# A hybrid decoder layer on one core: the second head of a recurrent chain in its own PSUM bank, three attention steps later, and the receptance-key product at the start of a stage

## The chip, the cores and the metric

The kernel runs on one core of a Trainium2 chip. The metric is the device time of one execution in microseconds (us). TensorE (PE) multiplies matrices from SBUF into PSUM, which has eight banks of 512 fp32 values for each of 128 rows; VectorE (DVE) and ScalarE (ACT) empty PSUM; GpSimd (POOL) does small element-wise work; SyncE (SP) issues most transfers.

## The reference

A decoder layer over 512 tokens and 16 meta tokens, width 1024, in fp32. The parts that matter here are the RWKV-7 time mixing and the windowed attention, which are merged by gates:

```python
proj = h @ w_in[l]
q, k, v, zr, gate_att, gate_rwkv = jnp.split(proj, [...], axis=-1)
att = lax.map(lambda qkv: swa_one(..., sinks_l), (q, k, v))       # scores + bias, softmax with a sink, times v
rw = rwkv7_time_mix(zr, ...)
merged = jax.nn.sigmoid(gate_att) * att + jax.nn.sigmoid(gate_rwkv) * rw
...
# inside rwkv7_time_mix, 16 heads of 64, for each token:
S = S * w_t + (S @ -kk_t) (kk_t * a_t)^T + v_t k_t^T ;  y_t = S @ r_t
bonus = jnp.sum(rh * kh * r_k, -1, keepdims=True) * vh            # receptance times keys
y = (groupnorm(y) * lnx_g + lnx_b + bonus) * g
```

After the merge come `w_out`, a normalization, a squared-ReLU MLP of width 4096 and a last normalization.

## The kernel before

Every fp32 matrix is split into a rounded part and a remainder, so a product is three matmuls (`three`, lines 340 to 342). The input projection is cut into *units* of 128 columns (keys, receptances, values, query, two gates of one pair of heads); a unit is a generator that issues matmuls into one of two banks `dps` and hands each finished bank to an `evict` function.

The 16 heads are worked on as 8 pairs, one pair per *stage*, the first head of a pair in rows 0 to 63 and the second in rows 64 to 127. The recurrence is cut into 8 chunks of 64 tokens. A stage s carries, interleaved with the units of the pairs ahead:

- the *solve* of pair s-1: filling up the inverses (`rwkv_blocks`, bank tag `Y`), the meta tokens' state (`rwkv_start`, bank tag `ch`), folding (`rwkv_fold`), then the *chain*, seven steps that carry the state from chunk to chunk (`rwkv_chain`), the outputs (`rwkv_outputs`, bank tag `Y`) and the norm;
- the *scan* of pair s: scores of keys and receptances (`rwkv_scores`), the inverse of 16x16 blocks on VectorE (`rwkv_inverse`, tiles `ftmp` and `Xf`), the bonus (`rwkv_bonus`, matmuls `bp`, lines 608 and 609), turns of scores, keys and values;
- the projections of pair s+1 (`rwkv_begin`, `rwkv_lora`, tiles `tw` and `ta`), the attention scores of pair s-1 (`attention_scores`, matmuls `sp`), the gate product (`gate_out`, matmuls `gp`) and, in stages 1 and 5, the turned attention values of a new group (`turn_heads`, matmuls `vp`).

A step of the chain multiplies two matrices, one per head (line 948), and `follow` scales the results into the next state Z: the first head on VectorE (line 906), the second on ScalarE (line 908). Both halves are in one bank, `ch`.

`weave` sets the order of TensorE's work: each item has a due time in microseconds of dense matmuls since the stage began, and units are stepped until that time is reached. TensorE's order is as written (`manual_schedule`). The order on the other engines is made when the program is built, by priority among what is ready; `ahead(n)` raises the priority. The order within an engine is then fixed, and each engine works in order.

The banks: two `dn` (units), two `pg` (tag `g`), one `ch`, one `Y`, two `pat` (tag `a`). Tag `a` serves `rwkv_lora`, `turn_heads`, the attention scores and the gate product in turn. In SBUF, `at` holds tiles for the attention: the split query `qhi` and `qlo` have the tags `sph` and `spl`, with one buffer each, and `sph` also holds the split keys and the values `va` of the attention early on. `evict` of `aside_query` writes qhi on ScalarE (line 1071) and qlo on VectorE (line 1072); four transfers take them to `qs`.

At the end of the receptance unit `rwkv_reads` makes the product rk (line 594, VectorE), its rounded part rkh (line 599, ScalarE) and the remainder rkl (line 600, VectorE); `rwkv_bonus` reads them in the next stage.

Of the kernel before, what the change touches and what calls it, by code (L numbers as in the profile page):

```python
# [11 lines left out]
F32 = mybir.dt.float32  # L12
F32R = mybir.dt.float32r
I32 = mybir.dt.int32
AF = mybir.ActivationFunctionType
ALU = mybir.AluOpType
# [4 lines left out]
P = 128  # L21
D = 1024
KT = D // P
SEQ = 512
NMETA = 16
T = SEQ + NMETA
# [3 lines left out]
C = 64  # L30
NCH = SEQ // C
# [50 lines left out]
PS = (2, 2, 1, 1, 2)  # L82
# [48 lines left out]
def hybrid_layer_kernel(ctx: ExitStack, tc: tile.TileContext, I: dict, out: bass.AP):  # L131
    nc = tc.nc
    dve, act, pool, pe = nc.vector, nc.scalar, nc.gpsimd, nc.tensor
# [6 lines left out]
    pch = ppr.enter_context(tc.tile_pool(name="pch", bufs=1, space=PSUM, side="right"))  # L140
# [3 lines left out]
    @contextmanager  # L144
    def ahead(n):

        now = tc.cur_priority
        tc.cur_priority = now - n
        yield
        tc.cur_priority += n  # L150
# [48 lines left out]
    def vcol(name, j):  # L199
        return vc[:, ROW0[name] + j : ROW0[name] + j + 1]  # L200
# [203 lines left out]
    at = p2.enter_context(tc.tile_pool(name="at", bufs=1))  # L404
    pew = ctx.enter_context(ExitStack())
    ew = pew.enter_context(tc.tile_pool(name="ew", bufs=1))
# [58 lines left out]
    ER = [slice(0, 64), slice(64, 128)]  # L465
# [120 lines left out]
    def rwkv_reads(j, r):  # L586
        S = SS[j]
        AXg = S["AX"].rearrange("p c k e t -> p e c k t")
        rx = c64(r)
        for e in range(2):  # L590
            R = slice(e * HD, (e + 1) * HD)
            dve.tensor_tensor(AXg[R, e, :, 1, :], rx[R], S["Px"][R, :, 1:], op=ALU.mult)
        rk = ew.tile([P, SEQ], F32, name="rk", tag="rk")
        dve.scalar_tensor_tensor(
            rk, r[:, NMETA:], vcol("r_k", j), S["kp"][:, NMETA:], op0=ALU.mult, op1=ALU.mult
        )
        rkh = ew.tile([P, SEQ], F32R, name="rkh", tag="rkh")
        rkl = ew.tile([P, SEQ], F32R, name="rkl", tag="u")
        act.copy(rkh, rk)
        dve.tensor_tensor(rkl, rk, rkh.bitcast(F32), op=ALU.subtract)  # L600
        S["rk"] = rkh, rkl
# [298 lines left out]
    def follow(S, c, src, last):  # L900

        Z, PC = S["Z"], S["PC"]
        for e in range(2):
            dst, scale = Z[c][ER[e], e, :], PC[ER[e], last : last + 1]
            if e == 0:
                dve.tensor_scalar(dst, src[ER[e]], scale, None, op0=ALU.mult)  # L906
            else:
                act.activation(dst, src[ER[e]], AF.Copy, scale=scale)  # L908

    def rwkv_start(j, n):  # L910

        S = SS[j]
        if n == 0:
            S["meta"] = pch.tile([P, 512], F32, name="meta", tag="ch", bufs=PS[2])
            S["RHm"] = rw.tile([NMETA, 2, HD], F32, name="RHm", tag="RHm", bufs=2)
        ps, RHm = S["meta"], S["RHm"]
        p6 = [ps[:, q * C : (q + 1) * C] for q in range(6)]
        m = slice(0, NMETA)
        with ahead(PRI["start"]):
            if n == 0:  # L920
                for e in range(2):
                    pe.matmul(
                        p6[e][m], S["AKm"][:, e, :], S["SVm"][:, e, :], start=True, stop=True
                    )
                act.copy(RHm.rearrange("p e i -> p (e i)"), ps[m, 0 : 2 * C])
            if n == 1:
                for e in range(2):
                    pe.matmul(p6[2 + e][m], S["XTm"][:, e, :], RHm[:, e, :], start=True, stop=True)
                for e in range(2):
                    act.copy(S["SVm"][32 * e : 32 * e + NMETA, e, :], p6[2 + e][m])  # L930
            if n == 2:
                for e in range(2):
                    pe.matmul(
                        p6[4][ER[e]], S["BTm"][:, e, :], S["SVm"][:, e, :], start=True, stop=True
                    )
                follow(S, 0, p6[4], NCH)

    def rwkv_chain(j, c):

        S = SS[j]  # L940
        Z, GQ = S["Z"], S["AX"]
        if c == 0:
            ch = pch.tile([P, 512], F32, name="ch", tag="ch", bufs=PS[2])
            S["st"] = [ch[:, d * C : (d + 1) * C] for d in range(NCH)]
        st = S["st"]
        with ahead(PRI["chain"]):
            for e in range(2):
                pe.matmul(st[c][ER[e]], GQ[:, c, 0, e, :], Z[c][:, e, :], start=True, stop=True)  # L948
            follow(S, c + 1, st[c], c)

    def rwkv_outputs(j):
# [319 lines left out]
    for n, pools in enumerate((((dn, "dn"), (pat, "a")), ((pg, "g"), (pch, None)))):  # L1271
        for b in range(4):
            pool_, tag = pools[b // 2]
# [44 lines left out]
    SS = [{} for j in range(PAIRS)]  # L1318
# [8 lines left out]
    def reads(j):  # L1327
        unit(f"r{j}", COL_R + j * P, shifted(COL_R + j * P, j, "r", partial(rwkv_reads, j), RSP))
# [35 lines left out]
    j = PAIRS - 1  # L1364
# [18 lines left out]
    F = partial  # L1383

    def scan(j):

        need = (f"k{j}", f"r{j}", f"v{j}")
        return [
            (0.0, need, F(rwkv_scores, j, 0)),
            (3.2, (), F(rwkv_meta, j)),  # L1390
            (3.2, (), F(rwkv_scores, j, 1)),
            (3.2, (), F(rwkv_inverse, j)),
            (5.6, (), F(rwkv_bonus, j)),
            (12.4, (), F(rwkv_turn_scores, j)),
            (18.6, (), F(rwkv_turn_keys, j)),
            (16.0, (), F(rwkv_inverse_place, j)),
            (23.2, (), F(rwkv_turn_values, j)),
        ]
# [19 lines left out]
    def project_in(j):  # L1418
        return [
            (0.0, (), F(rwkv_begin, j)),  # L1420
            (7.4, (), F(rwkv_lora, j, 0)),
            (8.6, (), F(rwkv_lora, j, 1)),
            (25.5 if j == 1 else 18.6, (f"k{j}",), F(rwkv_sums, j)),
        ]

    def attend(j, t0):
        return [(t0, (f"q{j}",), F(attention_scores, j, 0))] + [
            (t0 + t, (), F(attention_scores, j, 1 + i)) for i, t in enumerate((0.0, 2.8, 4.4))
        ]

    def attend_out(j, t0, t1, t2):
        return [
            (t0, (), F(attention_turn, j, 0)),
            (t1, (), F(attention_out, j, 0)),
            (t1, (), F(attention_turn, j, 1)),
            (t2, (f"ga{j}",), F(attention_out, j, 1)),
        ]

    def join(j, t0, t1, t2):
        return [  # L1440
            (t0, (f"gr{j}",), F(gate_out, j)), (t1, (), F(merge_rwkv, j)), (t2, (), F(merge, j)),
        ]

    with tc.manual_schedule(engines={mybir.EngineType.PE}):
        for s in range(-1, PAIRS + 1):
            if s <= PAIRS:
                units[:] = [u for u in all_units[: marks[s + 1]] if u[0] not in finished]
            items = []
            if s > 0:
                items += solve(s - 1)  # L1450
            if 0 <= s < PAIRS:
                items += scan(s)
            if s == -1:
                items += [
                    (0.0, (), F(rwkv_begin, 0)),
                    (9.0, ("wa",), F(rwkv_lora, 0, 0)),
                    (10.4, (), F(rwkv_lora, 0, 1)),
                    (20.0, ("k0",), F(rwkv_sums, 0)),
                ]
            if 0 <= s < PAIRS - 1:  # L1460
                items += project_in(s + 1)
            if s == 0:
                items += [(18.0, ("av",), F(aside_heads, 0))]
            if s == 4:
                items += [(26.0, (), F(aside_heads, 1))]
            if s in (1, 5):
                items += [(8.6, (), turn_heads)]
            if 0 < s < PAIRS - 1:
                items += attend(s - 1, 9.2) + join(s - 1, 11.6, 25.4, 0)[:2]
            if 1 < s < PAIRS:  # L1470

                items += attend_out(s - 2, 0.0, 4.6, 6.4) + join(s - 2, 0, 0, 7.0)[2:]
            if s == PAIRS - 1:
                items += [(10.0, (), merged_before)]
                items += attend(s - 1, 10.0) + attend_out(s - 1, 20.5, 22.9, 25.3)
                items += join(s - 1, 11.6, 26.5, 26.5)
                items += attend(s, 16.5)
                items += [(27.2, (), F(load_out, q, 0)) for q in range(3)]
            if s == PAIRS:
                items += attend_out(s - 1, 3.0, 5.4, 7.8) + join(s - 1, 0.0, 24.5, 25.5)  # L1480
                items += [(2.0, (), F(merged, s - 2)), (25.6, (), F(merged, s - 1))]
                items += [(3.0, (), residual_gain), (17.0, (), first_up)]
                items += [(3.0 + 3 * b, (), F(residual_rows, b)) for b in range(4)]
            weave(items, True)
# [182 lines left out]
    for half in range(2):  # L1667
# [14 lines left out]
        for n in range(2):  # L1682
            ns = slice(n * 512, (n + 1) * 512)
            acc = project(half * NF, NF, fhi, flo, n, HOLD if half and n else 2, ffp)
            for b in range(4):
                dve.scalar_tensor_tensor(
                    res[b][:, ns], res[b][:, ns], 1.0 if half else ALPHA, acc[b],
                    op0=ALU.mult, op1=ALU.add,
# [58 lines left out]
```

## Time and profile before

| | |
|---|---|
| median of 3 runs | 985.71 us (983.71 to 985.78) |
| profiled execution | 984.06 us, span 982.3 us |
| TensorE busy | 940.8 us, 96% |
| VectorE busy | 655.2 us, 67% |
| ScalarE busy | 455.7 us, 46% |
| GpSimd busy | 47.8 us, 5% |
| chain that ended last | PE 72%, DVE 17%, ACT 4%, DMA 2% |

How to read the views: a timeline row has the start, the duration, the engine, the line and operation, what is written from what, and in brackets the idle time of the engine before it with the instruction that ended it. A row of the waits has the total, the number of times and the longest. Matmul durations are modelled and overlap; two matmuls follow one another at the distance of their starts.

### The profile page before, as it was taken

The page shows a single profiled execution, that of the slowest core. Times are in us where ns is not written, and L with a number is a line of the kernel's source. Part 1 is how long each engine was busy: PE and PEld are TensorE (multiplying, and loading weights), DVE is VectorE, ACT ScalarE, POOL GpSimd, SP SyncE. Part 2 cuts the span into 40 slices and gives each one's busy share as a digit, 9 for nine tenths or more (in the row PEclk, how much of TensorE's full clock was granted, in tenths as well). Part 3 has the DMA queues.
Part 4 walks back from the last instruction along what each step waited for, and adds up shares of the span by engine and source line. Part 5 has one row for each costly group of instructions (what it writes and reads, how often), then busy time and mean ns, then how long its engine had stood idle before and what let it go on. Part 6 is the DMA issues. An engine that isn't in the chain of part 4 may idle for free.

```text
span 982.3 us, 19147 instructions
## 1 busy us (share of the span) xinstructions
PE 940.8 (96%) x7557; PEld 787.7 (80%) x7557; DVE 655.2 (67%) x1505; ACT 455.7 (46%) x1130; POOL 47.8 (5%) x108
## 2 busy tenths in 40 slices
PE   4989999999999999999998999999999999999996
PEld 3889878788887887887876778988888888888885
DVE  8677888877977788778876957566423244452427
ACT  6636457465474654745736724644321133432220
POOL 2001000010000100100001001000000000000001
PEclk9999999999999999999999999999999999999998
DMA  7546323223333332242434635133322323222222
GB/s 273 95 130 166 86 75 103 79 71 109 87 91 100 104 98 79 65 111 78 144 108 105 206 119 214 44 129 107 104 89 91 103 87 107 86 95 98 79 94 85
DMA packets 82674, 105.47 MB, mean 107 GB/s; under 512 B 47766, under 2 KB 54664, under 8 KB 82584
## 3 DMA queue, kind: packets, MB, share of 16 engines
q1 hardware_dynamic: 81088, 102.16, 34.3%
q10 hardware_dynamic: 1496, 2.08, 0.6%
q8 instruction: 59, 0.97, 0.4%
q14 instruction: 31, 0.25, 0.1%
HBM read 86.29 MB, written 13.74 MB: 102 GB/s over the span
## 4 chain that ended last, share of the span: by engine, by line
PE 72%; DVE 17%; ACT 4%; DMA 2%; issue 2%; POOL 2%; SPq 0%; DVEq 0%; ACTq 0%
PE dps L340 12%; PE dps L341 11%; PE dps L342 11%; PE acc L1516 6%; PE acc L1518 6%; PE acc L1517 6%; DVE wlo L259 3%; PE sc L668 2%; PE o L1290 1%; PE av L1194 1%; PE ch L948 1%; PE wp L873 1%; PE o L1291 1%; PE o L1292 1%; POOL grs L971 1%
## 5 line engine op out<-in xcount | busy, mean ns | idle before, releaser
L259 DVE TENSOR_TENSOR wlo<-wraw,whi 128x512 fp32r<-128x512 f32 x240 | 157.3, 686 | 168.3 <-ACT whi L256 167.6
L256 ACT CAST whi<-wraw 128x512 fp32r<-128x512 f32 x240 | 140.5, 617 | 266.3 <-PE dps L341 132.2
L340 PE MATMUL dps<-hhi,whi 128*128 128x264 f32 (+1 forms) x640 | 216.5, 338 | 4.5 <-DVE qlo L1072 2.8
L341 PE MATMUL dps<-hlo,whi 128*128 128x264 f32 (+1 forms) x640 | 203.5, 318 | 1.3 <-DVE hlo L321 1.3
L342 PE MATMUL dps<-hhi,wlo 128*128 128x264 f32 (+1 forms) x640 | 203.0, 317 | 0.4 <-DVE wlo L259 0.4
L340 PEld LDWEIGHTS dps<-hhi,whi 128*128 128x128 f32 x640 | 120.5, 188 | 19.4 <-DVE qlo L1072 4.1
L342 PEld LDWEIGHTS dps<-hhi,wlo 128*128 128x128 f32 x640 | 120.5, 188 | 9.0 <-DVE wlo L259 0.6
L341 PEld LDWEIGHTS dps<-hlo,whi 128*128 128x128 f32 x640 | 120.7, 189 | 7.5 <-DVE hlo L321 2.1
L341 PE MATMUL dps<-h1lo,whi 128*128 128x512 f32 (+1 forms) x256 | 97.5, 381 | 0.0
L340 PE MATMUL dps<-h1hi,whi 128*128 128x512 f32 (+1 forms) x256 | 97.5, 381 | 0.0
L342 PE MATMUL dps<-h1hi,wlo 128*128 128x512 f32 (+1 forms) x256 | 97.5, 381 | 0.0
L342 PEld LDWEIGHTS dps<-h1hi,wlo 128*128 128x128 f32 x256 | 48.1, 188 | 10.3
L341 PEld LDWEIGHTS dps<-h1lo,whi 128*128 128x128 f32 x256 | 48.1, 188 | 10.2
L340 PEld LDWEIGHTS dps<-h1hi,whi 128*128 128x128 f32 x256 | 48.1, 188 | 10.1
L1516 PE MATMUL acc<-whi,hhi 128*128 128x512 f32 x128 | 50.6, 395 | 0.0
L1517 PE MATMUL acc<-wlo,hhi 128*128 128x512 f32 x128 | 50.4, 394 | 0.0
L1518 PE MATMUL acc<-whi,hlo 128*128 128x512 f32 x128 | 50.2, 392 | 0.0
L1518 PE MATMUL acc<-whi,flo 128*128 128x512 f32 x112 | 44.1, 393 | 0.0
L1516 PE MATMUL acc<-whi,fhi 128*128 128x512 f32 x112 | 43.8, 391 | 0.0
L1517 PE MATMUL acc<-wlo,fhi 128*128 128x512 f32 x112 | 43.8, 391 | 0.0
L908 ACT ACTIVATE Z<-ch,PC 64x64 f32<-64x64 f32 x56 | 17.3, 310 | 36.4 <-DVE Z L906 35.7
L1616 DVE TENSOR_TENSOR rl<-rl 128x512 f32<-128x512 f32 (+1 forms) x36 | 22.8, 632 | 14.6 <-ACT hhi L1615 8.6
(302 smaller groups left out, 1732.7 us busy)
## 6 DMA issues: line engine op xcount, KB each, us to landing
wraw<-in_w_ff_dram SPq DMA_DIRECT2D x64, 512.0 KB, 3.6
wraw<-in_w_in_dram SPq DMA_DIRECT2D x52, 512.0 KB, 3.5
wraw<-in_w_out_dram SPq DMA_DIRECT2D x8, 512.0 KB
xt<-in_x_dram SPq DMA_DIRECT2D x4, 512.0 KB, 7.3
Nd<-NT SPq DMA_DIRECT2D x16, 128.0 KB, 2.9
bv<-bv SPq DMA_DIRECT2D x8, 256.0 KB, 2.1
bvm<-bv SPq DMA_DIRECT2D x8, 256.0 KB
qs<-qhi SPq DMA_DIRECT2D x16, 128.0 KB, 4.1
```

The lines of the kernel that those rows point to most:

```text
L256: act.copy(hi[:n, qs], raw[:n, qs])
L259: dve.tensor_tensor(lo[:n, qs], raw[:n, qs], hi[:n, qs].bitcast(F32), op=ALU.subtract)
L340: pe.matmul(ps, whi, xhi, start=first, stop=False)
L341: pe.matmul(ps, whi, xlo, start=False, stop=False)
L342: pe.matmul(ps, wlo, xhi, start=False, stop=last)
L668: pe.matmul(scs[e][:, c * P : (c + 1) * P], BK[ER[e], 4 * i + c, :], AXg[ER[e], e, 4 * i + c], start=True, stop=True,)
L873: pe.matmul(w4[:, c, :], XB[:, 4 * i + c, :], S["AT"][:, 4 * i + c, :], start=True, stop=True,)
L908: act.activation(dst, src[ER[e]], AF.Copy, scale=scale)
L1516: pe.matmul(acc[b], xhi[k][:, bs], hi[:, ws], start=first, stop=False)
L1517: pe.matmul(acc[b], xhi[k][:, bs], lo[:, ws], start=False, stop=False)
L1518: pe.matmul(acc[b], xlo[k][:, bs], hi[:, ws], start=False, stop=last)
L1616: dve.tensor_tensor(r, r, r, op=ALU.mult)
```

## The change

1. `rwkv_chain` takes a second bank, `ch2`, with tag `Y`. The first head's products go to `ch`, the second's to `ch2`; `follow` gets a pair of sources. In `rwkv_start` both sources stay the same bank.
2. The three operations rk, rkh and rkl leave `rwkv_reads` for a new function `rwkv_products`, called right after the first scores of the next stage. rk gets tag `sph`, the tile of the split query, in place of tag `rk`.
3. In the stages 1 to 6 the attention scores move by 1.4 us of dense matmuls, and so does the gate product; in the stages 1 and 5 `turn_heads` does too. Stage 7 keeps its times.

```diff
@@ rwkv_reads
-        rk = ew.tile([P, SEQ], F32, name="rk", tag="rk")
-        dve.scalar_tensor_tensor(
-            rk, r[:, NMETA:], vcol("r_k", j), S["kp"][:, NMETA:], op0=ALU.mult, op1=ALU.mult
-        )
+        S["r"] = r
+
+    def rwkv_products(j):
+
+        S = SS[j]
+
+        rk = at.tile([P, T], F32, name="rk", tag="sph")[:, :SEQ]
         rkh = ew.tile([P, SEQ], F32R, name="rkh", tag="rkh")
         rkl = ew.tile([P, SEQ], F32R, name="rkl", tag="u")
+        dve.scalar_tensor_tensor(
+            rk, S["r"][:, NMETA:], vcol("r_k", j), S["kp"][:, NMETA:], op0=ALU.mult, op1=ALU.mult
+        )
         act.copy(rkh, rk)
@@ follow
-                dve.tensor_scalar(dst, src[ER[e]], scale, None, op0=ALU.mult)
+                dve.tensor_scalar(dst, src[e][ER[e]], scale, None, op0=ALU.mult)
             else:
-                act.activation(dst, src[ER[e]], AF.Copy, scale=scale)
+                act.activation(dst, src[e][ER[e]], AF.Copy, scale=scale)
@@ rwkv_start
-                follow(S, 0, p6[4], NCH)
+                follow(S, 0, (p6[4], p6[4]), NCH)
@@ rwkv_chain
             ch = pch.tile([P, 512], F32, name="ch", tag="ch", bufs=PS[2])
-            S["st"] = [ch[:, d * C : (d + 1) * C] for d in range(NCH)]
+
+            ch2 = pch.tile([P, 512], F32, name="ch2", tag="Y", bufs=PS[3])
+            S["st"] = [[b[:, d * C : (d + 1) * C] for b in (ch, ch2)] for d in range(NCH)]
...
-                pe.matmul(st[c][ER[e]], GQ[:, c, 0, e, :], Z[c][:, e, :], start=True, stop=True)
+                pe.matmul(st[c][e][ER[e]], GQ[:, c, 0, e, :], Z[c][:, e, :], start=True, stop=True)
@@ scan
             (0.0, need, F(rwkv_scores, j, 0)),
+            (0.0, (), F(rwkv_products, j)),
@@ the stages
-                items += [(8.6, (), turn_heads)]
+                items += [(10.0, (), turn_heads)]
             if 0 < s < PAIRS - 1:
-                items += attend(s - 1, 9.2) + join(s - 1, 11.6, 25.4, 0)[:2]
+                items += attend(s - 1, 10.6) + join(s - 1, 13.0, 25.4, 0)[:2]
```

## The prediction

> **What bounds the kernel.** I read the page first, then the waits of TensorE, then the timeline around each kind of wait. The times in the views are one profiled execution of 984.06 us with this span and this load of TensorE:
>
> ```profile
> span 982.3 us, 19147 instructions
> PE 940.8 (96%) x7557; PEld 787.7 (80%) x7557; DVE 655.2 (67%) x1505; ACT 455.7 (46%) x1130; POOL 47.8 (5%) x108
> ```
>
> TensorE is the bound, and it takes its instructions in the order in which they are written. No edit removes a matmul, so only idle time of TensorE can be won or lost. The waits view names it (us in total, times, longest):
>
> ```profile
> PE ch L948 <- ACT Z L908: 3.4, 5, 1.4
> PE dps L340 <- DVE qlo L1072: 2.8, 6, 0.5
> PE sp L1136 <- ACT ta L500: 2.7, 4, 0.7
> PE vp L1052 <- issue: 1.5, 1, 1.5
> PE vp L1052 <- ACT ta L500: 1.5, 1, 1.5
> ACT Z L908 <- DVE Z L906: 35.7, 36, 2.2
> ```
>
> The first five rows are 11.9 us in four places, and each of the three parts of the change touches at least one of them. The sixth shows ScalarE standing behind VectorE in the chain. A median from three runs settles about 0.2%, or 2 us, for this kernel.
>
> **Receptance times keys (rk), moved out of the end of a stage.** The end of the stage from 168 to 231 us, TensorE first, then VectorE, then ScalarE:
>
> ```profile
> 227.17 0.28 PE L341 MATMUL dps<-hlo,whi 128*128 128x264 f32 x1
> 227.29 0.28 PE L342 MATMUL dps<-hhi,wlo 128*128 128x264 f32 x1
> 228.02 0.39 PE L340 MATMUL dps<-hhi,whi 128*128 128x264 f32 x1 [0.45 <-DVE qlo L1072]
> 225.21 0.75 DVE L594 SCALAR_TENSOR_TENSOR rk<-r,vc,kp 128x512 f32<-128x512 f32 x1
> 227.27 0.69 DVE L1072 SCALAR_TENSOR_TENSOR qlo<-dps,qhi 128x512 fp32r<-128x512 f32 x1
> 229.08 0.69 DVE L600 TENSOR_TENSOR rkl<-rk,rkh 128x512 fp32r<-128x512 f32 x1
> 225.99 0.62 ACT L599 CAST rkh<-rk 128x512 fp32r<-128x512 f32 x1 [1.21 <-DVE rk L594]
> 226.64 0.60 ACT L1071 ACTIVATE qhi<-dps 128x512 fp32r<-128x512 f32 x1
> ```
>
> Matmuls of this shape follow one another every 0.12 us (227.17 to 227.29); this one comes after 0.73, so a wait that shows 0.45 us of idle time costs 0.61, the rest being restart. Six times: 6 x 0.61 = 3.7 us. The bank that TensorE wants is freed by qlo, qlo waits for qhi, and qhi stands in ScalarE's queue behind rkh, which idles 1.21 us for rk. Without rk and rkh there, qhi can start up to 1.2 us earlier and qlo follows it. It is needed 0.7 us earlier than it comes, so the whole wait goes: **-3.7 us**. Next late there are the two products that merge z, which TensorE does not wait for.
>
> The same work, 0.75 + 0.69 us on VectorE and 0.62 on ScalarE, goes to the start of the next stage. Its cover:
>
> ```profile
> 239.50 0.28 DVE L906 TENSOR_SCALAR Z<-meta,PC 64x64 f32<-64x64 f32 x1 [1.52 <-PE meta L933]
> 243.48 0.68 DVE L685 TENSOR_TENSOR AX<-sc,con 64x512 f32<-64x512 f32 x1
> 245.62 0.69 DVE L1180 TENSOR_TENSOR pown<-pt,con 128x512 f32<-128x512 f32 x1 [1.45 <-ACT pall L1179]
> 246.39 0.39 PE L609 MATMUL bp<-rkl,bones 128*128 128x512 f32 x1
> qs<-qhi SPq DMA_DIRECT2D x16, 128.0 KB, 4.1
> ```
>
> VectorE is idle for 1.52 us before 239.50 and 1.45 us before 245.62; rk fits the first, rkl the second, and rkl is wanted only at 246.39. So I cost the move at nothing in the ordinary stages. Without that cover it costs TensorE up to the 2.1 us of the three operations at bp, per stage. rk now also waits until the split query has left the tile: the transfers land 4.1 us after issue and qhi ends at 227.24, so at 238 that wait is long over. Nothing new is queued on SP. What could be stuck behind a waiting rk on VectorE is the evacuation of the scores, with the inverse behind it.
>
> Stage 0 has no such room. Its second scores are evacuated just ahead of bp, and the value tile va takes the place of rk:
>
> ```profile
> 75.36 0.68 DVE L685 TENSOR_TENSOR AX<-sc,con 64x512 f32<-64x512 f32 x1
> 75.93 0.40 PE L609 MATMUL bp<-rkl,bones 128*128 128x512 f32 x1
> ```
>
> If all three operations run after 76.04, rkl is done at 78.1 and bp loses 2.2 us; if rk and rkh slip in earlier, under 1. Once: **+1.5 us** (0 to 2.2).
>
> **Scores, gate product and turned values later.** In the ordinary stages the scores of the attention need a bank that ScalarE frees with ta, and in two stages the turned values need it:
>
> ```profile
> 255.13 0.40 PE L342 MATMUL dps<-hhi,wlo 128*128 128x512 f32 x1
> 255.68 0.84 ACT L500 ACTIVATE ta<-dps,drv 128x264 f32<-128x264 f32 x2
> 256.20 0.39 PE L1136 MATMUL sp<-khi,qs 128*128 128x256 f32 x1 [0.67 <-ACT ta L500]
> 381.35 0.28 PE L499 MATMUL dps<-za,llo 128*128 128x264 f32 x1
> 383.10 0.49 PE L1052 MATMUL vp<-con,vT 64*128 64x64 f32 x5 [1.47 <-ACT ta L500]
> ```
>
> The scores lose 1.07 - 0.12 = 0.95 us, four times, 3.8 us; the turned values 1.75 - 0.12 = 1.63, twice, 3.3 us. The due times move by 1.4 us of dense matmuls. For the scores that is more than the wait, and fold(1) now stands ahead of them as well: **-3.8 us**. For the turned values 0.2 to 0.3 us stay: **-2.8 us**. These two instructions wait for the evacuation of the projection, and nothing that feeds it is moved. ScalarE's softmax of the stage ends later by as much; its result is turned only in the next stage.
>
> What the shift costs lies in the chain. VectorE is full there, and the order of its work changes:
>
> ```profile
> 190.00:200.00 10.00, 9.32 (x78) 7.71 (x76) 9.83 (x33) 5.46 (x14) 0.00 (x0) 1.00 0.06 16
> L1149 DVE TENSOR_REDUCE mx<-sb 128x8 f32<-128x1024 f32 x8 | 9.6, 1203 | 0.0
> ```
>
> (Columns of the first: span of the window, then TensorE, weight loads, VectorE, ScalarE, GpSimd.) The evacuation of the first two scores now falls between fold(1) and the first chain step. The last scores come between steps 3 and 4, so the 1.2 us reduction falls among the last steps, which are 0.95 us apart. In return the gate product and the third scores stand between steps 1 and 2, where the wait at 394.29 (below) is. A step caught behind the whole reduction is late by up to 1.0 us, in six stages: 0 to 6 us. Since the chain goes ahead of everything that is ready, I take a quarter: **+1.5 us**.
>
> **The second head in a bank of its own.** Two of the chain's five waits, and the group of the outputs' matmuls:
>
> ```profile
> 393.63 0.27 DVE L906 TENSOR_SCALAR Z<-ch,PC 64x64 f32<-64x64 f32 x1
> 393.93 0.31 ACT L908 ACTIVATE Z<-ch,PC 64x64 f32<-64x64 f32 x1 [1.16 <-DVE Z L906]
> 394.29 0.33 PE L948 MATMUL ch<-Z,AX 128*64 128x64 f32 x3 [0.64 <-ACT Z L908]
> 524.86 0.27 DVE L906 TENSOR_SCALAR Z<-ch,PC 64x64 f32<-64x64 f32 x1
> 525.46 0.60 ACT L1098 ACTIVATE ga<-dps 128x512 f32<-128x512 f32 x1
> 526.08 0.31 ACT L908 ACTIVATE Z<-ch,PC 64x64 f32<-64x64 f32 x1
> 526.44 0.34 PE L948 MATMUL ch<-Z,AX 128*64 128x64 f32 x4 [1.44 <-ACT Z L908]
> L962 PE MATMUL Y<-Z,AX 128*64 128x64 f32 x256 | 9.2, 225 | 0.0
> ```
>
> ScalarE starts 0.03 us after VectorE ends. With two banks it no longer stands behind VectorE, and the next step needs only VectorE's half, which was done at 393.90 and 525.13. With 0.05 us to start, the steps come at 393.95 and 525.18: 0.34 and 1.26 us earlier. Four waits of the first kind and one of the second: **-2.6 us**. What stays late is VectorE, whose half waits in its queue. The lower bound is nothing (ScalarE's place in its own queue decides), the upper one all five waits, 3.4 + 5 x 0.16 = 4.2 us. The new bank is that of Y, so the outputs can begin only when ScalarE has read the last step; they needed that result for their last quarter before, and 1.3 us of dense work lie between. I cost that at nothing; without that work it is up to three quarters of the outputs' 9.2 / 8 = 1.15 us, so 0.9 us in each of 8 stages.
>
> Is it the bank that makes ScalarE wait? The two halves lie in different rows of the bank and of Z.
>
> ```profile
> 236.70 1.10 ACT L837 COPY XB<-up 16x128 f32<-16x128 f32 x4 [2.18 <-PE up L831]
> 237.09 0.89 DVE L841 STREAM_TRANSPOSE X<-XB 32x256 f32<-32x256 f32 x2
> ```
>
> Here VectorE reads some rows of XB while ScalarE still writes others, so a tile in SBUF shared by two engines does not order them, and Z would not. The bank remains. [...]
>
> **Sum.** -3.7 - 3.8 - 2.8 - 2.6 = -12.9; +1.5 + 1.5 = 3.0; together -9.9: 984.06 - 9.9 = 974.2. The median of the runs, 985.71, is 1.65 above the profiled execution, so on the scale of the medians **975.8 us**. Its own bounds: with all four waits gone at 3.7 + 3.8 + 3.3 + 4.2 = 15.0 and nothing new 970.7; with 2.2 and 6 us new 981.0.
>
> **Rivals.** (1) *The chain's order is not the bank's.* ScalarE still follows VectorE, the 2.6 us stay: 978.4. For it speaks that the rows differ; against it XB. (2) *The wait moves on.* VectorE is 98% busy in the middle of a stage, so what TensorE saves it waits for a little later, and half of the 12.9 comes back: 975.8 + 6.5 = 982.3. Against it: each removed wait hangs on one evacuation and its place in a queue, and VectorE has the two idle pieces above. (3) *Slower: rk comes late.* VectorE's order is fixed when the program is built. If rk is put behind the second scores and pown, it starts at 246.3, rkl ends 2.1 us later at 248.4, and bp waits 2.0 us in each of 7 stages: 975.8 + 14.0 = 989.8. It turns the sign from 1.4 us a stage, that is with rk later than 245.7. For it: rk ranks below the scores, and its tile must be free. Against it: at 238 VectorE has nothing else to do.
>
> **Chances.** Forecast 0.58, rival 1 0.10, rival 2 0.18, rival 3 0.13, something else 0.01. The range 970.0 to 983.0 takes in the forecast's bounds and the first two rivals. Faster by over 0.2% is the forecast, rival 1 and most of rival 2: 0.81; within 0.2% the rest of rival 2: 0.06; slower 0.13.
>
> **What would show it.** No wait of dps for qlo at the end of stages 1 to 6; none of sp for ta; vp down to 0.3 us; L908 beginning together with L906 and its 35.7 us gone; rk near the meta state's step and before 240 in the stage's time; stages shorter by some 1.5 us. Wrong: a wait of bp for rkl in every stage, the chain waiting for L906 behind L1149, or Y waiting for L908.

## The result, and the profile after

The changed kernel takes 1003.6 us (median of 6 runs, 1000.37 to 1006.65) beside 985.75 (983.71 to 987.5) of the kernel before on the same chip: ratio 1.018, 95% interval 1.0162 to 1.0198 (the intervals further down are of the same kind). It is 18 us slower where 10 us less were forecast. Three views of the profiled execution (1006.65 us, the longest of the six, at a mean clock of 0.982 where the six have 0.982 to 0.989) say where to look: its size and load, the mean granted TensorE clock with the span (the kernel before has 982.3 us and 0.997 there), and the rows of the waits that answer to those quoted in the prediction, with the largest new ones.

```profile
span 1004.9 us, 19130 instructions
PE 956.6 (95%) x7557; PEld 798.9 (80%) x7557; DVE 655.7 (65%) x1505; ACT 454.7 (45%) x1130; POOL 47.4 (5%) x108
```

```profile
core 0: 1004.9 us, clock 0.982
```

```profile
PE up L852 <- DVE X L847: 15.4, 9, 2.9
PE sp L1144 <- DVE sb L1147: 2.3, 2, 2.1
PE dps L340 <- DVE qlo L1080: 1.9, 6, 0.3
DVE rk L602 <- DMA qs<-qhi: 29.7, 6, 5.3
ACT Z L914 <- PE ch L956: 44.7, 39, 2.0
ACT whi L256 <- DMA wraw<-in_w_in_dram: 23.1, 7, 4.3
```

Nearly everything that was to go is gone. TensorE's waits on the chain's scaled state (3.4 us) and on ta (2.7 for sp, 1.5 + 1.5 for vp) have no row any more; ScalarE waits for the chain's own matmul now (L914 for `ch`), not for VectorE; the wait on qlo went only from 2.8 to 1.9 us. Three rows are new or larger: the inverse's matmuls wait for X, rk waits for the transfers out of its tile, and the casts of the input weights wait for their loads (4.3 us before).

The 22.6 us between the two profiled spans close in two sums. TensorE's idle time (span less busy) went from 41.5 to 48.3 us, +6.8: 15.0 us on X and 1.1 on `sb` came in (2.3 where 1.2 was before) and 3.4 + 2.7 + 3.0 + 0.9 = 10.0 went out; 0.7 us are left without a row. Its busy time went from 940.8 to 956.6, +15.8, with the same 7557 matmuls: they ran at a lower clock. The mean clock says the same, (1 - 0.982) x 1004.9 = 18.1 us of clock lost against (1 - 0.997) x 982.3 = 2.9 before.

The start of the stage at 231 us, first VectorE of the kernel before, then VectorE of the changed one with the TensorE row that waits:

```profile
232.54 0.48 DVE L415 SCALAR_TENSOR_TENSOR v<-dps,vc,v 128x263 f32<-128x263 f32 x1
233.54 0.85 DVE L676 TENSOR_TENSOR NT<-sc,dv 64x256 f32<-64x256 f32 x2
237.09 0.89 DVE L841 STREAM_TRANSPOSE X<-XB 32x256 f32<-32x256 f32 x2
```

```profile
231.08 0.68 DVE L1080 SCALAR_TENSOR_TENSOR qlo<-dps,qhi 128x512 fp32r<-128x512 f32 x1
232.28 0.48 DVE L415 SCALAR_TENSOR_TENSOR v<-dps,vc,v 128x263 f32<-128x263 f32 x1
237.99 0.75 DVE L602 SCALAR_TENSOR_TENSOR rk<-r,vc,kp 128x512 f32<-128x512 f32 x1 [5.23 <-DMA qs<-qhi]
239.39 0.48 DVE L415 SCALAR_TENSOR_TENSOR v<-dps,vc,v 128x263 f32<-128x263 f32 x1
241.00 0.85 DVE L682 TENSOR_TENSOR NT<-sc,dv 64x256 f32<-64x256 f32 x2
244.54 0.89 DVE L847 STREAM_TRANSPOSE X<-XB 32x256 f32<-32x256 f32 x2
245.11 1.12 PE L852 MATMUL up<-X,NT 32*32 32x32 f32 x22 [2.88 <-DVE X L847]
```

rk stands between the two parts of the value mix, ahead of the scores, and holds all that follows for 5.23 us. X comes at 244.54, 13.5 us after qlo began, where the kernel before takes 9.8 (qlo at 227.27, X at 237.09). TensorE stands still for 2.88 us. Then a second thing happens. Windows of 2 us over the same place one stage earlier (length; busy time of TensorE, its weight loads, VectorE, ScalarE and GpSimd; granted clock; share of the DMA engines; GB/s):

```profile
172.00:174.00 2.00, 1.68 (x8) 1.05 (x6) 1.96 (x5) 1.33 (x6) 0.00 (x0) 1.00 0.61 188
174.00:176.00 2.00, 0.00 (x0) 0.00 (x0) 1.99 (x5) 0.00 (x0) 0.00 (x0) 1.00 0.18 74
176.00:178.00 2.00, 1.55 (x39) 1.39 (x40) 0.64 (x2) 0.13 (x1) 0.00 (x0) 0.59 0.03 8
178.00:180.00 2.00, 2.00 (x18) 1.33 (x15) 1.09 (x6) 1.28 (x5) 0.41 (x3) 0.50 0.02 5
180.00:182.00 2.00, 2.00 (x14) 1.68 (x13) 0.76 (x2) 0.04 (x1) 0.00 (x0) 0.50 0.01 1
```

TensorE starts nothing between 174 and 176, and from 176.4 on it is granted half its clock for 6.8 us. The queue of SP while rk waits, and a window of 2 us in the middle of that wait:

```profile
230.59 0.33 SPq L277 DMA_DIRECT2D wraw<-in_w_in_dram  x1
231.02 0.51 SPq L1089 DMA_DIRECT2D qs<-qhi  x1
231.79 0.51 SPq L1089 DMA_DIRECT2D qs<-qlo  x1
232.39 0.55 SPq L1089 DMA_DIRECT2D qs<-qhi  x1
```

```profile
234.00:236.00 2.00, 2.00 (x79) 1.73 (x77) 0.00 (x0) 0.00 (x0) 0.00 (x0) 1.00 1.07 217
```

A weight load of 512 KB is issued just ahead of the four transfers of the split query, and the DMA engines are full (1.07) while rk waits for the second qhi, issued at 232.39. My theory after this reading: rk's place and its tile make X late, the load beside the transfers makes rk's wait long, and the clock doubles the bill.

### The profile page after: what moved, and what is told of

It reads as the page before. It is cut to its first block, busy times and chain, and to the rows that moved or that the text cites. A ratio compares the mean times of both kernels' runs of the same rounds, so it can differ in the third digit from the quotient of the medians.

```text
span 1004.9 us, 19130 instructions
## 1 busy us (share of the span) xinstructions
PE 956.6 (95%) x7557; PEld 798.9 (80%) x7557; DVE 655.7 (65%) x1505; ACT 454.7 (45%) x1130; POOL 47.4 (5%) x108
## 4 chain that ended last, share of the span: by engine, by line
PE 71%; DVE 17%; DMA 5%; ACT 3%; issue 2%; POOL 1%; SPq 0%; DVEq 0%; ACTq 0%; POOLq 0%
PE dps L340 12%; PE dps L341 11%; PE dps L342 10%; PE acc L1525 6%; PE acc L1527 6%; PE acc L1526 6%; DVE wlo L259 3%; DMA qs<-qhi 3%; PE gq L896 2%; PE av L1202 2%; PE o L1298 1%; PE wp L879 1%; PE ch L956 1%; PE sc L674 1%; PE o L1299 1%
## 5 line engine op out<-in xcount | busy, mean ns | idle before, releaser
L340 PE MATMUL dps<-hhi,whi 128*128 128x264 f32 (+1 forms) x640 | 219.0, 342 | 3.2 <-DVE qlo L1080 1.9
L341 PE MATMUL dps<-hlo,whi 128*128 128x264 f32 (+1 forms) x640 | 205.8, 322 | 1.4 <-DVE hlo L321 1.4
L914 ACT ACTIVATE Z<-ch,PC 64x64 f32<-64x64 f32 x56 | 17.4, 310 | 45.3 <-PE ch L956 44.7
L1625 DVE TENSOR_TENSOR rl<-rl 128x512 f32<-128x512 f32 (+1 forms) x36 | 22.8, 632 | 15.4 <-ACT hhi L1624 9.2
```

The lines of the kernel that those rows point to most:

```text
L340: pe.matmul(ps, whi, xhi, start=first, stop=False)
L341: pe.matmul(ps, whi, xlo, start=False, stop=False)
L914: act.activation(dst, src[e][ER[e]], AF.Copy, scale=scale)
L1625: dve.tensor_tensor(r, r, r, op=ALU.mult)
```

## Experiments

All ratios are against the kernel before, run on the same chip.

**Is it rk's tile?** e1 gives rk its own buffer again and leaves the rest of the change as it is written (the order built for VectorE follows: rk is back ahead of qlo, at 224.28 us where qlo starts at 226.86):

```
-        rk = at.tile([P, T], F32, name="rk", tag="sph")[:, :SEQ]
+        rk = ew.tile([P, SEQ], F32, name="rk", tag="rk")
```

> As the changed kernel, but rk keeps its old tile (tag rk) in place of the split query's. Theory A (rk waits in VectorE's fixed order for the transfers out of the split query, everything behind it is late, TensorE idles before up for X and its clock then drops): the wait of rk for qs, 29.7 us, is gone, no wait of up for X over 0.5 us, no stretch at a granted clock of 0.5 in the stages. In the built order rk stands at its old place ahead of qlo, so the wait of dps for qlo is back at about 0.6 us six times; time about 975 (985.7 less the chain's 4.1, the scores' 3.8 and the turned values' 3.3). Rival B (the 1.4 us of rk and rkl at the stage's start delay X wherever the tile is): about 990 or more, up still waits. Rival C (the bank or the later scores delay the solve): stays near 1003.

e2 keeps the tile and moves rk behind the transposes of X in VectorE's order:

```
+        if j: add_after(SS[j - 1]["xt"], first)   # order only, no wait; first = rk's instruction, xt = the transposes of X
-            (0.0, (), F(rwkv_products, j)),
+            (1.4, (), F(rwkv_products, j)),
```

> As the changed kernel, tile of the split query included, but an order without a semaphore makes rk follow VectorE's transposes X of the solve (products due at 1.4 in place of 0). Theory A: rk finds the transfers landed, waits under 0.3 us, up does not wait for X, and the qlo wait is gone as well: about 972 to 975. Rival B: X is no longer delayed by rk but the scores and bp are: bp waits for rkl or the meta state waits, 980 to 990. Rival C: near 1003, since the bank and the times are unchanged.

e3 is the kernel before with rk's move alone, e4 the changed kernel without it:

```
e3:  b for b in (ch, ch);  turn_heads 8.6, attend 9.2, join 11.6        (rk as changed)
e4:  b for b in (ch, ch2); turn_heads 10.0, attend 10.6, join 13.0      (rk as before)
```

> The kernel before with only the move of rk, rkh and rkl into the split query's tile. Theory A: the whole loss without the other gains: about 16 us of waits of up for X, the same half-clock stretches (about 15 us), less some 1 us at qlo: 1010 to 1018. Rival B: the same sign, but rk itself waits little for qs. Rival C: near 985, since bank and times are as before.

> The changed kernel with rk, rkh and rkl back at the end of the receptance unit: only the second bank and the later scores, gate product and turned values. Theory A: 974 to 976 (985.7 less 4.1, 3.8 and 3.3, with the qlo wait kept). Rival B: the same. Rival C: near 1003.

Measured: e1 983.53 (ratio 0.9969, 0.9954 to 0.9983), e2 980.14 (0.9952, 0.9925 to 0.9978), e3 986.37 (1.0007, 0.9988 to 1.0027), e4 985.91 (1.0002, 0.9983 to 1.002). Either way of taking rk's wait out of VectorE's queue takes the whole loss away, so the wait is its carrier. But the move alone costs nothing, though its tile is just as shared: rk waits 8.7 us in all in e3 and 29.7 in the changed kernel. And the rest of the change without the move gains nothing, which the forecast does not allow. The theory behind the four runs missed all its numbers (975, 972 to 975, 1010 to 1018, 974 to 976); of e3 the rival near 985 held. What e1 and e2 still lose shows in their waits: 5.9 us on qlo in e1, 4.2 on X in e2 (whose profiled execution, 984.65 us, is among the slower of its seven), and casts that wait 17.1 and 28.6 us for loads. The rows of e4 for the wait on qlo and for the casts:

```profile
PE dps L340 <- DVE qlo L1074: 6.0, 6, 1.0
ACT whi L256 <- DMA wraw<-in_w_in_dram: 26.1, 8, 4.9
```

**Which parts together?** The corners that were left, with the same edits: e12 is the changed kernel with the old times, e16 without the second bank; e5 is the kernel before with the bank alone, e6 with the times alone.

> The changed kernel with the old times for scores, turned values and the gate product; the chain's second bank and rk in the split queries' tile stay. Theory (the loss is rk's wait for the transfers of that tile, made long only by the later times): with the old times the scheduler puts the two transfers of the high halves next to each other on SyncE, as it did when rk alone was moved (wait of rk 8.7 us in all), so rk waits under 10 us in all instead of 29.7, the matmuls of the inverse wait under 2 us on X instead of 15.4, and the clock doesn't drop behind them. Time 985.9 less the chain's wait of some 3 us: 981 to 985. Rival (the second bank or the tile costs it, whatever the times): 998 to 1005, with X still 10 us or more late in sum.

> The changed kernel without the second bank: rk in the split queries' tile and the later times alone. Theory (tile and times together make the loss, the bank has no part in it): the transfers of qhi take about 5 us to land, rk waits 25 us or more in all, X is late by 12 us or more, half-clock stretches in most stages, and the chain's wait is back: 1000 to 1008. Rival (all three are needed): below 994, rk's wait under 15 us.

> The kernel before with the chain's second bank alone. The chain's wait on ScalarE behind VectorE (35.7 us) goes, and with it TensorE's wait of 3.4 us on the scaled states. Theory of the prediction (those 3 us are on the path): 982 to 984. Rival (the scores' and turned values' waits, which come later in the same stages, take it back, as the run with the bank and early times seems to show): 985 to 987, with the sp wait at 4 us or more instead of 2.7.

> The kernel before with the later times alone. Theory (the loads are late only where the second bank and the later times come together): casts wait under 8 us for loads of these weights, the sp and vp waits of 5.7 us go, the chain's wait grows to some 7 us as with products and times: 984 to 988. Rival (the later times alone make the loads late): the casts' wait is 17 us or more; the time does not tell the two apart, the wait does.

| kernel | casts' wait for loads of w_in | rk's wait | X's wait | median | ratio |
|---|---|---|---|---|---|
| before | 4.3 | none | 0.4 | 985.75 | 1 |
| bank (e5) | 4.6 | none | 0.4 | 987.66 | 1.0007 to 1.004 |
| times (e6) | 3.3 | none | 0.4 | 986.06 | 0.9996 to 1.0027 |
| rk (e3) | 3.2 | 8.7 | 1.1 | 986.37 | 0.9988 to 1.0027 |
| bank, rk (e12) | 4.9 | 9.2 | 0.9 | 988.97 | 1.0011 to 1.005 |
| times, rk (e16) | 4.0 | 10.9 | 2.8 | 990.24 | 1.0025 to 1.0064 |
| bank, times (e4) | 26.1 | none | 1.7 | 985.91 | 0.9983 to 1.002 |
| all (changed) | 23.1 | 29.7 | 15.4 | 1003.6 | 1.0162 to 1.0198 |

My expectation of e16 was wrong and its rival right: it takes all three. The loads are late only where the second bank and the later times come together; the rk move then meets them. (The theories of e12, 981 to 985, and of e5, 982 to 984, missed too.) No part gains anything by itself, and the waits of e5 and e6 show where what they save goes:

```profile
PE dps L340 <- DVE qlo L1074: 5.5, 6, 0.9
PE sp L1138 <- DVE sb L1141: 2.1, 1, 2.1
```

```profile
PE ch L948 <- ACT Z L908: 6.6, 12, 1.4
PE dps L340 <- DVE qlo L1072: 5.0, 6, 0.8
```

With the bank alone (first fence) the chain's 3.4 us on ScalarE are gone, 0.6 on VectorE's half have come, and the waits on qlo (2.8 before) and sb (1.2) are 3.6 longer. With the times alone (second fence) 5.7 us on ta are gone; the chain's wait (3.4 before) and qlo's are 5.4 longer. What TensorE does not wait for in one place it mostly waits for in the next. These waits are not the whole account of the spans: the profiled execution of e5 (990.38 us, the second longest of its twelve) also has three stretches of 3.4 us at half clock, that of the kernel before none on its record until the last microseconds.

**What makes the transfers slow?** First ScalarE, before (upper three rows) and changed (lower three):

```profile
217.50 0.62 ACT L256 CAST whi<-wraw 128x512 fp32r<-128x512 f32 x1
218.40 0.61 ACT L256 CAST whi<-wraw 128x512 fp32r<-128x512 f32 x1
220.82 2.16 ACT L1164 ACTIVATE sb<-sb,sm 128x128 f32<-128x128 f32 x7 [1.13 <-DVE sm L1162]
```

```profile
222.43 0.60 ACT L256 CAST whi<-wraw 128x512 fp32r<-128x512 f32 x1
225.44 2.45 ACT L1172 ACTIVATE sb<-sb,sm 128x128 f32<-128x128 f32 x8
227.80 1.21 ACT L256 CAST whi<-wraw 128x512 fp32r<-128x512 f32 x2
```

The softmax, 1.4 us later, now has its scaling between the two casts of one weight. The raw weight's buffer comes free that much later, and the load that wants it stands on SP ahead of the transfers. e8 issues both transfers of qhi before those of qlo; e9 gives the weight loads a priority of 200 in place of 100, and e15 does so in stages 1 to 6 alone:

```
e8:   for d, src in enumerate((hi, lo)):        # loops exchanged
          for e in range(2): nc.sync.dma_start(qs[e]..., src...)
e9:   PRI["load"] = 200
e15:  PRI["load"] = 200 if 0 < s < PAIRS - 1 else 100
```

> The changed kernel with both transfers of the high halves (qhi) issued before those of the low halves, on SyncE; nothing else moves, VectorE's order is the same. Theory (rk stands still for the second transfer of qhi, and its lateness is what the inverse's matmuls wait for): the second transfer is issued one place, some 0.6 us, earlier and lands with fewer others beside it; rk's wait falls from 29.7 us to 20 to 25 in sum, the wait on X from 15.4 to 8 to 11, and where a gap gets shorter the clock drops less often: 985 to 998. Rival (rk's wait is for the engine's place, not for that transfer): X as late as before, 1002 to 1006.

> The changed kernel with the weight loads' priority at 200 in place of 100, so that on ScalarE the casts of the weights stand ahead of the softmax's scaling again and the raw weights' buffers come free and are refilled sooner; the transfers of qhi and qlo stay in their order. Theory of the late weights (the later softmax pushes the casts back, the loads come late, stand beside the transfers of the queries and hold v's evacuation and the weights' low halves): the wait of the casts for the loads falls from 23.1 us to under 8, and since nothing large lies beside the transfers rk waits 10 to 20 us instead of 29.7: 980 to 993. Rival (the loads' lateness is hidden and rk's wait is the order of the transfers alone): the casts' wait falls, rk's does not, 1000 to 1005.

> The changed kernel with the weight loads' priority at 200 in stages 1 to 6 alone, so that the second cast of each weight stands ahead of the softmax's scaling on ScalarE and the raw buffer is refilled before the queries' transfers are issued; the start is as in the changed kernel, and VectorE's rk keeps its place. Theory (the load beside the transfers makes them slow): transfers of qhi land in 2.3 us instead of 5.1, rk waits under 10 us, X under 6 us, no half-clock stretch in stages 2 to 7: 984 to 988. Rival (the tile's wait costs it whatever the load does): rk over 20 us, over 998.

e8 changes nothing: 1004.23 (1.0156 to 1.0212), rk's wait 28.3 us. The order of the four transfers is not it. e9 takes 989.95 (1.0022 to 1.005), e15 986.49 (1.0001 to 1.0023); e9 moves the loads at the start of the kernel too, where TensorE then waits 4.3 us in a place where the others have no wait (`tm` for `xm`). SP and VectorE of e15 in that stage, and the DMA views' row for the transfers (median from issue to landing) in e15 and in the changed kernel:

```profile
223.46 0.34 SPq L277 DMA_DIRECT2D wraw<-in_w_in_dram  x1
229.20 0.51 SPq L1089 DMA_DIRECT2D qs<-qhi  x1
230.53 0.55 SPq L1089 DMA_DIRECT2D qs<-qhi  x1
233.81 0.75 DVE L602 SCALAR_TENSOR_TENSOR rk<-r,vc,kp 128x512 f32<-128x512 f32 x1 [2.12 <-DMA qs<-qhi]
```

```profile
qs<-qhi SPq DMA_DIRECT2D x16, 128.0 KB, 2.3
```

```profile
qs<-qhi SPq DMA_DIRECT2D x16, 128.0 KB, 5.1
```

The load is issued 5.7 us ahead of the transfers, not 0.4; the second qhi lands in 233.81 - 230.53 = 3.3 us, not 237.99 - 232.39 = 5.6; rk waits 8.4 us in all. The DMA engines are busy for 0.62 of the window from 232 to 234 us, in which e15's rk waits, not 1.07. With rk still ahead of the scores, 17 of the 18 us are gone.

**What is the clock's share?** e7 adds matmuls that nothing reads just ahead of those that wait for X, for the pairs 1 to 6 (j), whose solves lie in the stages 2 to 7:

```
+                if 1 <= j <= 6:
+                    for q in range(24):
+                        pe.matmul(up[:, 256:512], bones, hhi[:, q % KT, 0:256], start=True, stop=True)
```

> The changed kernel with 24 more matmuls of 128x256 (a constant by part of the activations, into a part of the bank that nothing reads) in stages 1 to 6 just ahead of the matmuls that wait for X, where TensorE stands idle for 2.4 to 3.3 us; by the pitch of the 128x512 matmuls (0.235 us) they take 24 x 0.118 = 2.8 us a stage. Theory of the clock (the idle gap makes the granted clock fall to half for 3.4 or 6.8 us, which costs some 15 us of the 18): the gaps are filled, no stretch at half clock follows, and the kernel with more work is faster: 986 to 992. Rival (the wait on X alone costs it, and the clock's fall is a mark and no cost): no change, 1002 to 1008, the filler lying in time that was idle anyway.

It is faster with more work: 995.93 (1.0068 to 1.011) against 1003.6. Its load, clock and wait on X:

```profile
PE 962.6 (97%) x7701; PEld 808.7 (81%) x7701; DVE 655.8 (66%) x1505; ACT 455.0 (46%) x1130; POOL 47.4 (5%) x108
```

```profile
core 0: 996.8 us, clock 0.995
```

```profile
PE up L856 <- DVE X L848: 1.3, 5, 0.6
```

rk still waits 29.9 us. 144 more matmuls at an estimated 0.118 us (matmuls of 256 columns follow one another every 0.12 us at 256.42 us in the kernel before) are 17.0 us of work, so by this estimate the old matmuls took 962.6 - 17.0 = 945.6 us, 11.0 less than in the changed kernel, and the idle time fell by 14.1. 17.0 - 11.0 - 14.1 = -8.1, the difference of the spans 996.8 and 1004.9. The expected 986 to 992 left out that the filler adds these 17.0 us where only 14.1 were idle; two stretches of 3.4 us at half clock are also left.

**The faster version.** e13 has rk behind X as in e2, and the loads' priority as in e15; e14 is the control, the kernel before with that priority.

> The version in which rk stands behind the transposes of X on VectorE (980.1), and in stages 1 to 6 the weight loads' priority at 200 in place of 100, so that the casts stand ahead of most of the softmax's scaling on ScalarE; the start keeps 100. Theory of the late weights (they are what still makes X late, 4.2 us in that version, and holds v's evacuation): the casts' wait for the loads falls from 28.6 us to under 10, X's wait from 4.2 us to 1 to 2, and the kernel takes 974 to 979, the fastest so far. Rival (with rk out of the way the loads' lateness is hidden, and the casts put VectorE's or ScalarE's other work back instead): 979 to 985.

> Control: the kernel before with that same priority of 200 in stages 1 to 6. Its casts wait only some 8 us for loads, so there is little to win: 984 to 988. Below 982 the priority would be a gain of its own, and what it gives to the changed kernel no sign of what the change had cost.

e13 takes 977.24 us (976.24 to 979.35), ratio 0.9912 (0.989 to 0.9934), faster than both kernels; e14 986.08 (0.9989 to 1.0013). Of e13 the page, the clock, the wait on qlo, and VectorE around rk:

```profile
PE 940.8 (97%) x7557; PEld 787.9 (81%) x7557; DVE 657.2 (67%) x1505; ACT 454.7 (47%) x1130; POOL 47.3 (5%) x108
```

```profile
core 0: 974.5 us, clock 0.998
```

```profile
PE dps L344 <- DVE qlo L1086: 3.2, 6, 0.6
```

```profile
233.87 0.89 DVE L853 STREAM_TRANSPOSE X<-XB 32x256 f32<-32x256 f32 x2
234.80 0.75 DVE L606 SCALAR_TENSOR_TENSOR rk<-r,vc,kp 128x512 f32<-128x512 f32 x1
236.24 0.28 DVE L918 TENSOR_SCALAR Z<-meta,PC 64x64 f32<-64x64 f32 x1 [0.69 <-ACT rkh L611]
```

rk now sits in the idle time ahead of the meta state's step, without a wait, and X's wait has no row left. The four versions with the whole change (medians, from different chips; the kernel before takes 985.3 to 985.75 on them):

| | loads late | loads early |
|---|---|---|
| rk ahead of the scores | 1003.6 (changed) | 986.49 (e15) |
| rk behind X | 980.14 (e2) | 977.24 (e13) |

Early loads are worth 17 us where rk stands in front and 3 where it does not. Those 3 us are not sure from these runs: the intervals of e2 and e13 touch (0.9925 to 0.9978, 0.989 to 0.9934). The X rows are clear, 4.2 us in e2 and none in e13. The row of e2 and that of e15:

```profile
PE up L858 <- DVE X L853: 4.2, 12, 1.3
```

```profile
PE up L852 <- DVE X L847: 4.9, 13, 1.4
```

The time from the start of qlo to that of X, in the stages 2 to 7, shows how the two delays add: 9.8 us in the kernel before and in e13; 10.8 to 11.9 in e2, where only the late load is left (at 231 us VectorE waits 4.00 us there for a cast, and the cast for its load); 11.0 to 11.9 in e15, where only rk's shorter wait is left; 12.7 to 13.5 in the changed kernel. So the late load holds X by itself too, and by e2 part of rk's 5.23 us would have been waited for in any case. Either delay alone makes TensorE wait 0.7 to 0.8 us a stage, both together 2.6. The clock adds the rest: between 90 us and the last microseconds the profiled execution of e15 has no stretch at half clock, the changed kernel's has five.

## Why the prediction was wrong

**rk moved, -3.7 us: the step that failed.** I put rk into the 1.52 us of idle time before 239.50 because VectorE had nothing else to do there. That was a place in time and not in the queue. rk's inputs are ready long before, so the program's order put it ahead of the scores, where VectorE arrives at 232.76 us and the transfers were not over until 237.99. I named what stands behind ("the evacuation of the scores, with the inverse behind it") and left it at nothing. I also counted the 4.1 us from the first transfer; the tile is free only when the second has landed, which the kernel before issues 1.3 us later (227.27 and 228.60), and that 4.1 is the one landing that its trace holds for these 16 transfers. e2 and e13 put rk where I had drawn it, and there it costs no wait. "Nothing new is queued on SP" was true of the instructions and wrong of their order: the weight load moved to just ahead of the transfers. The gain at the end of the stage was mis-sized too. The wait on qlo fell to 1.9 us, not to nothing, and stands at 3.2 in e13: with rkh gone, the casts and the softmax's scaling are what qhi and qlo follow.

**Stage 0, +1.5 us, and the chain's new waits, +1.5 us:** neither came. bp waits for nothing in the changed kernel, and no matmul of the chain has a row among TensorE's waits. (The last steps, which I had 0.95 us apart by their due times, are 1.19 and 1.54 us apart in the trace.)

**Scores and turned values, -3.8 and -2.8 us:** the waits on ta went as said, vp's wholly, where 0.3 us were to stay. The first term was too large as worked out: the matmul ahead of the scores is one of 512 columns, and those follow one another every 0.23 us (254.67, 254.90, 255.13), not 0.12, so four waits cost 4 x 0.84 = 3.4 us. The wait on sb in the last stage is 2.1 us where 1.2 was before; e5, with the old times, has the same 2.1. What failed is the sentence that the softmax only ends later and is turned in the next stage. True of the softmax, but the weight casts share ScalarE's queue with it, and the weight loads hang on the casts.

**Second bank, -2.6 us:** the mechanism holds. ScalarE's 35.7 us behind VectorE went with the bank and stay in e16 and e6, which lack it (50.9 and 48.9 us there). All 3.4 us of the chain's wait went, the upper bound, but alone the bank brought no time: e5 is 0.07 to 0.4% slower than the kernel before.

**The sum.** -12.9 us was forecast for the four places and -9.9 in all. The -3.7 at qlo did not hold: e13, the fastest, waits 3.2 us there, where the kernel before waits 2.8. The other three, 3.8 + 2.8 + 2.6 = 9.2, add up only in e13, at 985.63 - 977.24 = 8.4 us (985.63 is the kernel before on that chip), after rk was ordered and the loads put back. In its profiled execution 3.4 + 2.7 + 3.0 = 9.1 us of waits are gone and 0.4 (qlo) and 1.1 (sb) have come, 7.6, where the span fell by 7.8.

**The rivals.** Rival 2, the wait that moves on, is what each part shows alone (e5, e6). Rival 3 had the right cause, rk, on the wrong side: not too late for bp, but too early in VectorE's order, so that X is late. Its price, 2.0 us a stage at bp, is nowhere; the 2.4 to 3.3 us from start to start at X took its place.

**The clock** is not in the prediction at all, and it is 11 to 15 us of the loss: by the estimate above the filler took 11.0 us of TensorE's busy time away, and the five stretches, 30.6 us at half clock, cost an estimated half of that, 15.3.

What stays open: why the program's order moves the cast behind the scaling only with bank and times together. The order is made when the program is built, and no trace shows how.

## What to carry to other kernels

An instruction that is moved and given a shared buffer has two new facts: what it waits for, and where the program's order puts it. Find the second in the queue of its engine before costing the move by a gap in time, and tie it down if what follows is wanted soon. A shift of work on one engine should be followed to the transfers: here a softmax 1.4 us later moved a cast, the cast a buffer, the buffer a load, and the load stood in front of the transfers that the moved instruction waited for.

## What the runs showed of the hardware

In the changed kernel the short idle times of TensorE cost more than they lasted: with the filler (e7) 14.1 us of idle time went, and with it an estimated 11.0 us of TensorE's busy time. The waits on X leave 3.06, 3.27, 2.56, 2.74, 2.40 and 3.30 us between two starts in stages 2 to 7 (the matmul ahead of the one shown at 245.11 starts at 241.84, hence 3.27), and by the trace's record of the granted clock half speed follows five of them, for 6.8 us (four times) or 3.4 us; the 2.74 us have none after them. So 2.40 us was followed by half speed and 2.74 us was not, and less was followed by it elsewhere, for 3.4 us each: 1.76 and 1.75 us between two starts in e3 (at 126.47 and 383.06), 1.83 in e14 (at 525.88). The kernel before has the same 1.83 us (at 524.62) and no half speed after them. So what counts besides the length of the idle time is not settled here, and no run gives a length that is safe.

The transfers out of the query's tile, 128 KB each, landed 2.3 us after issue (median, e15) with the weight load 5.7 us ahead of them, and 5.1 us (median, changed kernel) with a 512 KB load issued 0.4 us before the first. A trace holds the landing of few of the 16, three in each of these two: 2.2, 2.3 and 2.9 us in e15; 2.3 (at 84.8 us, where the load is 6.0 us ahead), 5.1 and 5.6 in the changed kernel. In the other runs with late loads (e1, e2, e4, e7, e8) the landings with the load 0.4 to 0.6 us ahead took 4.4 to 6.3 us.
